# Loading the first expert tiles during the second search, and giving half of its weight splits to GpSimd, in a one-core decoder block

## The chip, the core and the metric

The kernel runs on one core of a Trainium2 chip. Its engines work beside each other, each on its own queue of instructions: TensorE (PE in the profile; PEld is its weight load), VectorE (DVE), ScalarE (ACT) and GpSimd (POOL); SyncE (SP) issues most of the plain DMA transfers and GpSimd the gathers. The metric is the time of one execution on the device in microseconds (us), lower is better. 0.3% of it is 4.9 us.

## The reference, cut to what matters

One decoder layer on 512 tokens of width 1024, in float32. Three token mixers are merged and added to x; then comes a feed-forward of 16,384 single-neuron experts, of which each token takes 128: for each of 8 heads the best 16 pairs of two 128-key halves.

```
def peer_ffn(h, w_q, keys1, keys2, u, v):
    q = (h @ w_q).reshape(B, S, PEER_HEADS, 2, half)          # 8 heads
    s1 = einsum('bshd,hkd->bshk', q[..., 0, :], keys1)        # 128 scores for each half
    s2 = einsum('bshd,hkd->bshk', q[..., 1, :], keys2)
    v1, i1 = top_k(s1, 16);  v2, i2 = top_k(s2, 16)
    cand = (v1[..., :, None] + v2[..., None, :])
    sv, si = top_k(cand, 16)
    experts = e1 * N_KEYS + e2                                # 128 of 16384 for a token
    gates = softmax(sv)
    ...
        a = einsum('cd,ced->ce', h_c, u[e_c])
        act = gelu(a) * g_c
        return einsum('ce,ced->cd', act, v[e_c])
x = x + mixers(rmsnorm(x));  x = x + peer_ffn(rmsnorm(x), ...)
```

## The kernel before, in words

**Blocks and stages.** The 512 tokens are four blocks of 128. Blocks 0 and 1 are served row by row ("rows"): for each of their 128 choices GpSimd gathers one expert row per token (an indirect DMA, L833), and a step on VectorE uses it. The table `u` gives 128 dot products for each block (L843), the table `v` adds 128 weighted rows into the block's tile `mg` (L852), so there are 512 rows. Blocks 2 and 3 are served densely: all 128 tiles of `uT` (512 KB each) are multiplied with their tokens (`dense_u`, L968, 16 matmuls of 256 columns each), ScalarE puts the gelu into a slot of the tile `ga` (L970), the gates are spread over all experts, and 128 tiles of `v` follow (`dense_v`, L142 to L144).

By the trace the stages are: the mixers of block 0 up to about 170 us; the mixers of blocks 1 to 3 up to about 640 us, with block 0's search and rows beside; the second search, for blocks 1 to 3 together, from 640 to 768 us; a stretch that I call the cover, from 768 to 859 us, in which U tiles run on TensorE while VectorE turns the search's result into weights and expert numbers and takes 36 rows; the spread of the gates, up to about 1000 us; and the tail with the 128 V tiles, the U tiles from 57 and the remaining rows.

**The second search.** It is a loop over 8 heads (`search`). Each head has two tiles of `w_pq` of 512 KB. Such a tile goes the way of `load_split`: SyncE loads it into `raw` (a ring of three), ScalarE casts the upper part `whi` (L116), then the lower part `wlo = raw - whi` is made, on VectorE (L128) or on GpSimd (L126). The number `share[0]` decides which: it is added to a running sum at each tile, and each time that the sum passes 1, GpSimd makes the tile. In the second search it is 0. Then 24 matmuls give the query `qp`, six matmuls the scores `sc` (L720), ScalarE copies them (L723), VectorE finds the best 16 of each half (L678 to L682), GpSimd adds the pairs `cand` (L689), and VectorE finds the best 16 of those one head later. The scores run two heads ahead.

Two other things are written into this loop. While its steps' assumed costs add up, every `PER_ROW` of them one row of block 0's `v` table is taken "apart": ScalarE scales the gathered row and GpSimd adds it to `mg` (L849, the second way beside L852). And 8 U tiles (`FIRST_U`) are multiplied, whose loads go through the same `raw` ring. All rows of block 0 add into one tile `mg`, so they come one after another, whichever engine adds them.

**Buffers of U.** `soon` holds the first 52 slots of `ga`, 256 numbers per partition each; a U tile is as large as four slots. U tiles from the 8th on are loaded into a ring of six (`URING`), three in `hhi` and three in `hlo`, which are free only when the search's last matmul has read them.

**Order.** Up to the end of the second search a scheduler orders the instructions of all engines by their assumed times. From the line with `manual_schedule` on, GpSimd, VectorE and TensorE run in the order in which the code is written; SyncE and ScalarE stay with the scheduler. Each engine runs its queue in order.

Of the kernel before, what the change touches and what calls it, by code (L numbers as in the profile page):

```python
# [16 lines left out]
S, D, NB, KC = 512, 1024, 4, 8  # L17
# [4 lines left out]
NK = 128  # L22
# [5 lines left out]
ND = len(DENSE)  # L28
TD = 128 * ND
FIRST_U, COVER, DURING, AFTER = 8, 24, 25, 0  # L30
KEPT = FIRST_U + COVER
SPILT = (128 - KEPT) // 3
AMONG, UNWEIGHED = 1.0, 14
LAG = FIRST_U + COVER + DURING + AFTER
GA_LATE = 6
URING, URING_V = 6, 3
# [13 lines left out]
AHEAD, ROWS_IN, MORE = 4, 5, 2  # L50
LATER = 400
PACE = {"search": 9.0, "choose": 8.0, "rows": 3.5}
EARLY_ROWS, PER_ROW = 176, 4.6


@with_exitstack
def tile_block(ctx: ExitStack, tc: tile.TileContext, t: dict, out: bass.AP):
    nc = tc.nc
# [36 lines left out]
    due, share = [0.0], [0.0]  # L95
# [3 lines left out]
    def load_raw(src, n):  # L99
        loads[0] += 1  # L100
        pool = early[0] if early and loads[0] % (RAW_MORE + 3) >= 3 else wp
        raw = pool.tile([128, WSLOT], F32, tag="raw", name="raw")
        fill(raw, src, n)
        return raw
# [107 lines left out]
    def turn(xs, g, hi, lo, dg=None, tags=("tp", "sc")):  # L212

        w = 128 * len(xs)
        for dc in range(KC):
            ps = bank(tags[dc % len(tags)])
            for b, x in enumerate(xs):
                dst, src = ps[:, b * 128:(b + 1) * 128], x[:, dc * 128:(dc + 1) * 128]
                if dg is None:
                    PE.transpose(dst, src, ident)  # L220
                else:
                    PE.matmul(dst, src, dg[:, b], start=True, stop=True)
            A.activation(hi[dc], ps[:, :w], AF.Copy, scale=g[:, dc:dc + 1])
            if lo:
                V.scalar_tensor_tensor(lo[dc], ps[:, :w], g[:, dc:dc + 1], hi[dc].bitcast(F32),
                                       op0=OP.mult, op1=OP.subtract)
# [447 lines left out]
    def search(qq, h2T, f, nb, fetch=None):  # L674

        def top16(v, i, src, n):
            tmp = qq.tile([128, 128], F32, tag="tmp", name="tmp")
            V.max(v[:, 0:8], src)  # L678
            V.max_index(i[:, 0:8], v[:, 0:8], src)
            V.match_replace(tmp[:, :n], v[:, 0:8], src, -3.0e38)  # L680
            V.max(v[:, 8:16], tmp[:, :n])
            V.max_index(i[:, 8:16], v[:, 8:16], tmp[:, :n])  # L682

        pairs = {}

        def candidates(v12):
            cand = qq.tile([128, nb, NC], F32, tag="cand", name="cand")
            for i0, ni, nj, c0 in ROWS:
                G.tensor_tensor(cand[:, :, c0:c0 + ni * nj].rearrange("p b (i j) -> p b i j", j=nj),  # L689
                                v12[:, :, 0, i0:i0 + ni, None].to_broadcast([128, nb, ni, nj]),  # L690
                                v12[:, :, 1, None, :nj].to_broadcast([128, nb, ni, nj]), op=OP.add)
            return cand

        def top_pairs(h):
            if h not in pairs:
                return
            cand = pairs.pop(h)
            for b in range(nb):
                top16(f.best[:, b, h], f.pos[:, b, h], cand[:, b], NC)
                yield 1.2  # L700

        def scores(h):
            s = []
            keys = qq.tile([128, 2, NK], F32, tag="keys", name="keys")
            nc.sync.dma_start(keys, t["keysT"][:, 2 * h:2 * h + 2])
            qp = qq.tile([128, 2, 128 * nb], F32, tag="qp", name="qp")
            if nb == 1:
                q = qq.tile([128, 256], F32, tag="q", name="q")
                gemm_plain(h2T, halves(t["w_pq"][2 * h:2 * h + 2]), 256, lambda b, ps: A.copy(q, ps), fetch)
                ps = bank("tg")  # L710
                for half in range(2):
                    PE.transpose(ps[:, half * 128:(half + 1) * 128], q[:, half * 128:(half + 1) * 128], ident)
                A.copy(qp.rearrange("p i s -> p (i s)"), ps[:, :256])
            else:
                for half in range(2):
                    A.copy(qp[:, half], gemm_tr(h2T, t["w_pq"][2 * h + half]))
            for half in range(2):
                ps = bank("sc")
                for b in range(nb):
                    PE.matmul(ps[:, b * 128:(b + 1) * 128], qp[:, half, b * 128:(b + 1) * 128], keys[:, half],  # L720
                              start=True, stop=True)
                sc = qq.tile([128, nb, NK], F32, tag="s", name="s", bufs=2 * (deep + 1))
                A.copy(sc.rearrange("p b k -> p (b k)"), ps[:, :128 * nb])  # L723
                s.append(sc)
            return s

        deep = 1 if nb == 1 else 2
        ready = [scores(h) for h in range(deep)]
        for h in range(PH):
            s = ready.pop(0)  # L730
            if h + deep < PH:
                ready.append(scores(h + deep))
            v12 = qq.tile([128, nb, 2, TOPK], F32, tag="v12", name="v12")
            for b in range(nb):
                for half in range(2):
                    top16(v12[:, b, half], f.ids[half][:, b, h], s[half][:, b], NK)
                    yield 1.6
            yield from top_pairs(h - 1)
            pairs[h] = candidates(v12)
        yield from top_pairs(PH - 1)  # L740
# [178 lines left out]
    gq, acc, late, v_raw, u_raw = {}, {}, [], {}, {}  # L919
# [4 lines left out]
        return soon[:, s] if s <= LAG - GA_LATE else late[0][:, s - (LAG + 1 - GA_LATE)]  # L924

    def fetch_u(k):
        if not FIRST_U <= k < NK:
            return
        s = (k - FIRST_U) % URING if k < LAG else (k - LAG + 1) % URING_V
        if s % BIG == 0:  # L930
            if k - FIRST_U < URING:
                u_ring[s // BIG] = by_token(wide(("hhi", "hlo")[s // BIG], BIG))
        u_raw[k] = u_ring[s // BIG][:, s % BIG]
        nc.sync.dma_start(u_raw[k], t["uT"][k])

    u_ring, u_next = [None, None], [FIRST_U]

    def fetch_u_to(k):
        while u_next[0] <= min(k, NK - 1):
            fetch_u(u_next[0])  # L940
            u_next[0] += 1
# [3 lines left out]

    def dense_u(k):

        if k < FIRST_U:
            w = load_raw(t["uT"][k], D)[:, :D]
        else:  # L950
            fetch_u_to(min(k + URING - 1, LAG + 1) if k < LAG else k)
            w = u_raw.pop(k)
        if split_u(k):
            hi, lo = (gp[0].tile([128, D], F32R, tag=tag, name=tag, bufs=1) for tag in ("uhi", "ulo"))
            A.copy(hi, w)
            yield
            V.tensor_sub(lo, w, hi.bitcast(F32))
            yield
            ps, hi, lo = bank("mm"), *(x.rearrange("p (n w) -> p n w", n=KC) for x in (hi, lo))
            for dc in range(KC):  # L960
                mm3(ps[:, :TD], (hi[:, dc], lo[:, dc]), [x[dc] for x in h2s], dc == 0, dc == KC - 1)
            A.activation(ga(k), ps[:, :TD], AF.Gelu)
            return
        w = w.rearrange("p (n w) -> p n w", n=KC)
        yield
        ps = bank("mm")
        for dc in range(KC):
            PE.matmul(ps[:, :TD], w[:, dc], h2f[dc], start=dc == 0, stop=dc == KC - 1)  # L968
            yield
        A.activation(ga(k), ps[:, :TD], AF.Gelu)  # L970
# [5 lines left out]
    with tc.tile_pool(name="qb", bufs=2) as qq:  # L976
        turn([x1[b] for b in GROUPS[1]], g2, *h2T)
        spent, dg, credit[0] = 0.0, None, 0.0
        for cost in search(qq, h2T, f, BIG):
            spent += cost  # L980
            if dg is None and spent > 12.0:
                V.tensor_copy(rstd[:, 1:NB], factors(sums, BIG))
                dg = diagonals(rstd[:, 2:NB], ND)
                turn([x1[b] for b in DENSE], g2, h2f, None, dg)
            credit[0] += cost
            while credit[0] >= PER_ROW and NJ <= done[0] < known[0]:
                credit[0] -= PER_ROW
                with tc.high_priority(-LATER):
                    step(apart=True)
            if k_u < FIRST_U and spent > 104.0 / FIRST_U * (k_u + 1):  # L990
                list(dense_u(k_u))
                k_u += 1
    assert k_u == FIRST_U, (k_u, spent)

    cp = build.enter_context(tc.tile_pool(name="cp", bufs=1))
    ctx.enter_context(tc.manual_schedule(engines={mybir.EngineType.Pool, mybir.EngineType.DVE, mybir.EngineType.PE}))
# [158 lines left out]
    while k_u < LAG:  # L1155
        list(dense_u(k_u))
        k_u += 1
    start, ready = done[0], list(operands(0))[1]
    assert start >= 2 * NJ
    nc.sync.dma_start(out[0:128], x1[0])  # L1160
# [120 lines left out]
```

## Time and profile before

| what | value |
|---|---|
| time, median of 3 runs | 1629.26 us (1627.56 to 1631.83) |
| the profiled execution: its own time | 1624.32 us |
| its span in the trace | 1622.5 us |
| busy over the span: PE / DVE / ACT / POOL | 95% / 86% / 47% / 49% |
| DMA, mean | 328 GB/s, 531.83 MB |
| mean granted TensorE clock | 0.981 |

The profiled execution is 4.9 us shorter than the median, which is 0.3%; times inside it are given from the start of its span. Rows of the timeline give start, duration, engine, line, operation, the tile written and those read, how many, and in brackets how long the engine stood idle before and what released it. A table by windows gives the busy time of each engine in each stretch of the span.

### The profile page before, as it was taken

To read this page: it belongs to the slowest core of one execution; us is meant where nothing else is said; L and a number is where in the kernel's file an instruction comes from. 1 tells how busy PE (TensorE), PEld (TensorE's weight loads), DVE (VectorE), ACT (ScalarE), POOL (GpSimd) and SP (SyncE) were. 2 spreads that over 40 slices of the span, in tenths; PEclk is the share of its full clock that TensorE was granted. 3 is DMA by queue.
4 is the path that set the end of the run, shared out by engine and by line. 5 is a ranking of instruction groups with operands and counts; after the bars stand their busy time and mean duration, and the time that the engine had idled before them with its cause. 6 is when DMAs were issued, how large, how long until landed. Compare 5 with 4: busy or idle time off the path is not lost.

```text
span 1622.5 us, 26255 instructions
## 1 busy us (share of the span) xinstructions
PE 1545.8 (95%) x8934; PEld 1382.1 (85%) x8934; DVE 1394.1 (86%) x2709; ACT 769.1 (47%) x1770; POOL 790.5 (49%) x625
## 2 busy tenths in 40 slices
PE   6999999999998989987999999899999999998998
PEld 5999899998887988987888998688888888887887
DVE  5677358899988999999998999788899888897987
ACT  7787337645445434543117878333333333333332
POOL 1100012767556555678553332566555555555652
PEclk9999999999998999999999999999999999999999
DMA  7586743899998899867997999999999999999995
GB/s 298 197 276 219 252 162 131 319 356 319 339 317 296 294 345 347 291 212 258 348 393 286 362 386 335 402 399 379 390 397 402 397 400 402 401 401 401 383 400 220
DMA packets 178101, 531.83 MB, mean 328 GB/s; under 512 B 18224, under 2 KB 47152, under 8 KB 177968
## 3 DMA queue, kind: packets, MB, share of 16 engines
q0 software_dynamic: 73728, 268.47, 44.4%
q1 hardware_dynamic: 100784, 249.12, 42.1%
q10 hardware_dynamic: 3456, 12.58, 2.0%
q8 instruction: 70, 1.15, 0.3%
q14 instruction: 63, 0.52, 0.1%
HBM read 515.42 MB, written 14.68 MB: 327 GB/s over the span
## 4 chain that ended last, share of the span: by engine, by line
PE 51%; DMA 17%; issue 14%; POOL 9%; DVE 8%; ACT 2%; SPq 0%; POOLq 0%; DVEq 0%; ACTq 0%
PE mm L968 15%; DMA row<-in_peer_v_dram,eidx 9%; POOL row L833 8%; PE mm L143 5%; PE mm L142 5%; PE mm L144 5%; DMA row<-in_peer_u_dram,eidx 3%; PE mm L295 2%; DVE wlo L128 2%; DVE scr L843 2%; PE sc L1038 2%; PE tp L1038 2%; PE sc L143 1%; PE sc L144 1%; PE tp L144 1%
## 5 line engine op out<-in xcount | busy, mean ns | idle before, releaser
L833 POOL DMA_INDIRECT row<-in_peer_v_dram,eidx x256 | 351.2, 1372 | 280.8 <-DVE mg L852 157.3
L833 POOL DMA_INDIRECT row<-in_peer_u_dram,eidx x256 | 334.9, 1308 | 266.4 <-DVE scr L843 155.0
L128 DVE TENSOR_TENSOR wlo<-raw,whi 128x1024 fp32r<-128x1024 f32 (+1 forms) x243 | 305.7, 1259 | 44.4 <-ACT whi L116 34.9
L843 DVE SCALAR_TENSOR_TENSOR scr<-row,own 128x1024 bf16<-128x1024 f32 x256 | 314.5, 1229 | 23.1 <-DMA row<-in_peer_u_dram,eidx 20.1
L852 DVE SCALAR_TENSOR_TENSOR mg<-row,acts,mg 128x1024 f32<-128x1024 f32 x237 | 304.4, 1284 | 10.7 <-DMA row<-in_peer_v_dram,eidx 6.8
L968 PE MATMUL mm<-h2f,hhi 128*128 128x256 f32 x1168 | 266.3, 379 | 0.0
L968 PEld LDWEIGHTS mm<-h2f,hhi 128*128 128x128 f32 x1168 | 218.9, 190 | 30.0
L116 ACT CAST whi<-raw 128x1024 fp32r<-128x1024 f32 (+1 forms) x148 | 154.8, 1049 | 93.7 <-PE mm L143 38.7
L189 POOL TENSOR_TENSOR rsy<-rsv,mhalf 128x4 f32<-128x4 f32 (+5 forms) x25 | 39.3, 1576 | 218.2 <-DVE rsv L188 126.2
L1084 ACT CAST whi<-raw 128x1024 fp32r<-128x1024 f32 x96 | 100.5, 1047 | 71.5 <-DMA raw<-in_peer_v_dram 50.1
L142 PE MATMUL sc<-whi,ah 128*128 128x512 f32 x256 | 110.7, 433 | 11.3 <-ACT ah L1082 6.7
L142 PE MATMUL mm<-hhi,whi 128*128 128x384 f32 x320 | 111.1, 348 | 8.0 <-ACT ga L970 6.8
L970 ACT ACTIVATE ga<-mm 128x256 f32<-128x256 f32 x95 | 36.4, 383 | 172.0 <-PE mm L968 165.7
L143 PE MATMUL mm<-hlo,whi 128*128 128x384 f32 x320 | 111.5, 348 | 0.0
L144 PE MATMUL mm<-hhi,wlo 128*128 128x384 f32 x320 | 110.6, 346 | 0.0
L142 PE MATMUL mm<-whi,hhi 128*128 128x256 f32 (+1 forms) x360 | 104.6, 292 | 3.0 <-DVE g L572 1.9
L143 PE MATMUL sc<-wlo,ah 128*128 128x512 f32 x256 | 102.2, 399 | 4.6 <-DVE wlo L128 4.6
L143 PE MATMUL mm<-wlo,hhi 128*128 128x256 f32 (+1 forms) x360 | 103.1, 287 | 0.9 <-DVE wlo L128 0.9
L1082 ACT CAST ah<-ga 128x256 fp32r<-128x256 f32 x116 | 46.7, 405 | 118.6 <-PE tp L143 73.8
L144 PE MATMUL sc<-whi,al 128*128 128x512 f32 x256 | 102.3, 399 | 0.0
L144 PE MATMUL mm<-whi,hlo 128*128 128x256 f32 (+1 forms) x360 | 101.8, 285 | 0.0
L142 PE MATMUL tp<-whi,ah 128*128 128x512 f32 x256 | 101.4, 396 | 0.0
(289 smaller groups left out, 3780.7 us busy)
## 6 DMA issues: line engine op xcount, KB each, us to landing
hhi<-in_uT_dram SPq DMA_DIRECT2D x96, 512.0 KB
raw<-in_peer_v_dram SPq DMA_DIRECT2D x96, 512.0 KB
raw<-in_w_tr_dram SPq DMA_DIRECT2D x48, 512.0 KB
raw<-in_w_nat_dram SPq DMA_DIRECT2D x40, 512.0 KB
last<-in_peer_v_dram SPq DMA_DIRECT2D x32, 512.0 KB
raw<-in_w_o_dram SPq DMA_DIRECT2D x24, 512.0 KB
hlo<-in_uT_dram SPq DMA_DIRECT2D x24, 512.0 KB
gd<-st ACTq DMA_DIRECT2D x24, 512.0 KB
```

The lines of the kernel that those rows point to most:

```text
L116: A.copy(hi[:, :n * w], raw[:, :n * w])
L128: V.tensor_sub(lo, raw, hi.bitcast(F32))
L142: PE.matmul(ps, lh, rh, start=first, stop=False)
L143: PE.matmul(ps, lh, rl, start=False, stop=False)
L144: PE.matmul(ps, ll, rh, start=False, stop=last)
L833: G.indirect_dma_start(out=r, out_offset=None, in_=t["peer_" + tab], in_offset=bass.IndirectOffsetOnAxis(ap=eidx[b][:, j:j + 1], axis=0))
L843: V.scalar_tensor_tensor(scr, r, 1.0, h2n[b], op0=OP.mult, op1=OP.mult, accum_out=acts[b][:, c]))
L852: V.scalar_tensor_tensor(x1[b], r, acts[b][:, c], x1[b], op0=OP.mult, op1=OP.add))
L968: PE.matmul(ps[:, :TD], w[:, dc], h2f[dc], start=dc == 0, stop=dc == KC - 1)
L1038: PE.matmul(ps[:, u], o[:, 1, u], o[:, 0, u], start=True, stop=True)
L1082: A.copy(ah, a)
L1084: A.copy(hi, raw)
```

## The change

Two things change, and two numbers go with them.

**U tiles.** The first 13 U tiles (`PRE_U`) no longer go through the `raw` ring and the ring of six. Each is loaded into four slots of `soon` whose activations come much later, during the second search, and is read from there by its 16 matmuls. The ring of six starts at tile 13, and its tiles are requested one earlier than before around the spread.

**Lower parts.** From the fifth head (`POOL_HEADS`) `share[0]` is 1, so GpSimd makes 8 of the 16 `wlo` of the second search. `PER_ROW` goes from 4.6 to 6.0, which writes fewer rows apart into the search.

```
+PRE_U = 13
...
-EARLY_ROWS, PER_ROW = 176, 4.6
+EARLY_ROWS, PER_ROW = 176, 6.0
+POOL_HEADS = 4
...
             else:
+                share[0] = 1.0 if h >= POOL_HEADS else 0.0
                 for half in range(2):
                     A.copy(qp[:, half], gemm_tr(h2T, t["w_pq"][2 * h + half]))
...
     def fetch_u(k):
-        if not FIRST_U <= k < NK:
+        if k < PRE_U:
+            u_raw[k] = soon[:, 4 * k:4 * k + 4].rearrange("p a b -> p (a b)")
+            nc.sync.dma_start(u_raw[k], t["uT"][k])
             return
-        s = (k - FIRST_U) % URING if k < LAG else (k - LAG + 1) % URING_V
+        s = (k - PRE_U) % URING if k < LAG else (k - LAG + 1 + (LAG - 1 - PRE_U) % URING) % URING_V
...
-        if k < FIRST_U:
-            w = load_raw(t["uT"][k], D)[:, :D]
-        else:
-            fetch_u_to(min(k + URING - 1, LAG + 1) if k < LAG else k)
-            w = u_raw.pop(k)
+        if k >= FIRST_U:
+            fetch_u_to(min(max(k, PRE_U) + URING - 1, LAG) if k < LAG else k)
+        w = u_raw.pop(k)
...
+            if u_next[0] < PRE_U and spent > 6.0 * u_next[0] + 6.0:
+                fetch_u_to(u_next[0])
...
     assert k_u == FIRST_U, (k_u, spent)
+    share[0] = 0.0
...
         list(dense_u(k_u))
         k_u += 1
+    fetch_u_to(LAG + 2)
```

The lines behind the first edits move by two or three: the L128 of before is L130 now, L833 is L836, L849 is L852, L852 is L855, the ring's load L934 is L939, and the new load is L932. GpSimd's `wlo` is L128 in the changed kernel.

What the scheduler makes of it, engine by engine. SyncE at the start of the second search, before (rows with a number are the engine's queue in order; `raw` is the ring of three):

```order
L110 DMA raw_7733<-in_w_pq_dram 128x1024
L705 DMA keys_7572<-in_keysT_dram 128x256
L705 DMA keys_7651<-in_keysT_dram 128x256
L110 DMA raw_7765<-in_w_pq_dram 128x1024
L110 DMA raw_7862<-in_w_pq_dram 128x1024
L110 DMA raw_7894<-in_w_pq_dram 128x1024
L705 DMA keys_7730<-in_keysT_dram 128x256
L110 DMA raw_8003<-in_uT_dram 128x1024
```

The first row is the fifth tile of `w_pq`, the fourth row the sixth. The first U tile stands behind the eighth. The changed kernel at the same place:

```order
L112 DMA raw_7733<-in_w_pq_dram 128x1024
L707 DMA keys_7572<-in_keysT_dram 128x256
L707 DMA keys_7651<-in_keysT_dram 128x256
L932 DMA ga_7513<-in_uT_dram 128x1024 x8
L112 DMA raw_7765<-in_w_pq_dram 128x1024
L932 DMA ga_7513<-in_uT_dram 128x1024 x5
L112 DMA raw_7859<-in_w_pq_dram 128x1024
L112 DMA raw_7891<-in_w_pq_dram 128x1024
```

Eight U loads now stand ahead of the sixth `w_pq` tile and five behind it.

SyncE at the end of the search, before (the last U tile of the `raw` ring behind the ring of six):

```order
L110 DMA raw_8797<-in_uT_dram 128x1024
L934 DMA hlo_8914<-in_uT_dram 128x1024
L934 DMA hhi_8910<-in_uT_dram 128x1024 x3
L934 DMA hlo_8914<-in_uT_dram 128x1024 x2
L110 DMA raw_8880<-in_uT_dram 128x1024
```

In the changed kernel that last row does not exist, since U tile 7 has been in `soon` from the start of the search; the six ring loads follow the last keys.

GpSimd in the middle of the search, before (`row` gathers, `mg` adds, `cand` pair sums):

```order
L849 TENSOR_TENSOR mg0_2246<-mg0_2246,row_6691 128x1024
L689 TENSOR_TENSOR cand_7854<-v12_7809 128x3x8
L689 TENSOR_TENSOR cand_7854<-v12_7809 128x3x16
L689 TENSOR_TENSOR cand_8055<-v12_7938 128x3x24
L689 TENSOR_TENSOR cand_8055<-v12_7938 128x3x16
L833 DMA row_7850<-in_peer_v_dram,eidx0_176 128x1024
L849 TENSOR_TENSOR mg0_2246<-mg0_2246,row_6694 128x1024
```

The same first add in the changed kernel:

```order
L836 DMA row_7835<-in_peer_v_dram,eidx0_176 128x1024
L852 TENSOR_TENSOR mg0_2246<-mg0_2246,row_6691 128x1024
L128 TENSOR_TENSOR wlo_8096<-raw_8092,whi_8094 128x1024
L128 TENSOR_TENSOR wlo_8224<-raw_8220,whi_8222 128x1024
L691 TENSOR_TENSOR cand_8212<-v12_8136 128x3x8
L836 DMA row_8013<-in_peer_v_dram,eidx0_176 128x1024
L691 TENSOR_TENSOR cand_8212<-v12_8136 128x3x16
L852 TENSOR_TENSOR mg0_2246<-mg0_2246,row_6694 128x1024
```

The add of `row_6691` stood ahead of the third pair sum of the first head (`cand_7854`), and now stands behind the second of the third head (ahead of the third of `cand_8212`); two `wlo` queue right behind it. Over the whole search GpSimd has 8 `wlo` more and 16 adds where it had 19; behind its last pair sum stand three gathers with their adds, where one stood.

VectorE, the last of block 0's rows that it adds itself ahead of those adds, before:

```order
L681 MAX v12_7809<-tmp_7832 128x8
L128 TENSOR_TENSOR wlo_8067<-raw_8063,whi_8065 128x1024
L852 SCALAR_TENSOR_TENSOR mg0_2246<-row_6655,acts0_177,mg0_2246 128x1024
L680 MATCH_REPLACE tmp_7838<-v12_7809,s_7643 128x128
L682 MAX_INDEX ids1_7515<-v12_7809,tmp_7832 128x8
```

And in the changed kernel:

```order
L681 MAX_INDEX ids1_7515<-v12_8136,s_7807 128x8 x2
L855 SCALAR_TENSOR_TENSOR mg0_2246<-row_6652,acts0_177,mg0_2246 128x1024
L684 MAX_INDEX ids0_7514<-v12_8136,tmp_8137 128x8
L683 MAX v12_8136<-tmp_8144 128x8
L855 SCALAR_TENSOR_TENSOR mg0_2246<-row_6655,acts0_177,mg0_2246 128x1024
L682 MATCH_REPLACE tmp_8150<-v12_8136,s_7801 128x128
```

It is the 14th row in both. It stood in the first head's best-16 work (`v12_7809`) and now stands in the third head's (`v12_8136`). GpSimd's first add, of `row_6691`, adds to the same tile right after it. Behind the search the number of rows in the cover (36) and in the spread (51) is as before, and the tail takes 233 where it took 230. TensorE has 27 U tiles behind the search's last score in both kernels.

More of the change, by code (lines that the diff above doesn't have):

```diff
@@ L926, in fetch_u @@
     def fetch_u(k):
-        if not FIRST_U <= k < NK:
+        if k < PRE_U:
+            u_raw[k] = soon[:, 4 * k:4 * k + 4].rearrange("p a b -> p (a b)")
+            nc.sync.dma_start(u_raw[k], t["uT"][k])
             return
-        s = (k - FIRST_U) % URING if k < LAG else (k - LAG + 1) % URING_V
+        s = (k - PRE_U) % URING if k < LAG else (k - LAG + 1 + (LAG - 1 - PRE_U) % URING) % URING_V
         if s % BIG == 0:
-            if k - FIRST_U < URING:
+            if k - PRE_U < URING:
                 u_ring[s // BIG] = by_token(wide(("hhi", "hlo")[s // BIG], BIG))
@@ L934, in fetch_u @@
         nc.sync.dma_start(u_raw[k], t["uT"][k])
-    u_ring, u_next = [None, None], [FIRST_U]
+    u_ring, u_next = [None, None], [0]
     def fetch_u_to(k):
```

## The prediction

> **What bounds the kernel now.** I read the table by windows first, cut at the stages' borders, then around each border the chain that ended last, the timelines and the waits.
>
> ```profile
> span 1622.5 us, 26255 instructions
> ...
> core 0: us, PE busy (x) PEld busy (x) DVE busy (x) ACT busy (x) POOL busy (x), PEclk, DMA share, GB/s
> 654.00:690.31 36.31, 35.48 (x223) 34.70 (x222) 34.88 (x113) 20.44 (x32) 20.83 (x21) 1.00 0.84 296
> 690.31:768.64 78.33, 66.20 (x358) 61.01 (x356) 76.15 (x487) 31.44 (x49) 65.55 (x60) 0.97 0.68 233
> 768.64:859.00 90.36, 89.53 (x403) 78.19 (x403) 81.46 (x129) 13.62 (x31) 51.98 (x40) 0.97 0.96 371
> 859.00:1000.00 141.00, 139.24 (x881) 129.19 (x882) 141.00 (x197) 116.36 (x460) 46.51 (x46) 1.00 0.93 346
> 1240.00:1590.00 350.00, 338.72 (x1641) 286.64 (x1640) 309.60 (x374) 126.92 (x201) 199.55 (x133) 0.99 1.03 398
> ```
>
> VectorE is full in the search (76.15 of 78.33) and in the spread (141.00 of 141). TensorE is full in the cover and nearly so in the tail (338.72 of 350), where the DMA engines are full as well. The search's end and the cover decide here. First TensorE's side of that border (issue, matmuls, pieces of the chain, ScalarE):
>
> ```profile
> 756.61 0.33 SPq L110 DMA_DIRECT2D raw<-in_uT_dram  x1
> 756.61 12.14 DMA raw<-in_uT_dram
> 756.41 0.83 PE L720 MATMUL sc<-keys,qp 128*128 128x128 f32 x6
> 757.08 7.07 PE L968 MATMUL mm<-h2f,raw 128*128 128x256 f32 x32
> 768.88 3.33 PE L968 MATMUL mm<-h2f,raw 128*128 128x256 f32 x7 [4.73 <-DMA raw<-in_uT_dram]
> 775.24 0.39 ACT L970 ACTIVATE ga<-mm 128x256 f32<-128x256 f32 x1 [2.45 <-PE mm L968]
> 778.69 0.38 ACT L970 ACTIVATE ga<-mm 128x256 f32<-128x256 f32 x1 [3.07 <-PE mm L968]
> 858.12 0.38 ACT L970 ACTIVATE ga<-mm 128x256 f32<-128x256 f32 x1 [3.07 <-PE mm L968]
> ```
>
> The last U tile in the raw ring was issued at 756.61, behind the six ring loads, and landed 12.14 us later; TensorE waited 4.73 us for it. From then to 858.12 the U tiles follow one another every 3.45 us (775.24 to 778.69). Then VectorE's side:
>
> ```profile
> 768.16 0.91 DVE L747 TENSOR_TENSOR ex<-best 128x384 f32<-128x384 f32 x1
> 774.46 1.28 DVE L852 SCALAR_TENSOR_TENSOR mg<-row,acts,mg 128x1024 f32<-128x1024 f32 x1
> 851.69 2.59 DVE L852 SCALAR_TENSOR_TENSOR mg<-row,acts,mg 128x1024 f32<-128x1024 f32 x2
> 859.00 4.62 DVE L1023 TENSOR_TENSOR o<-tg,eT 128x1024 f32<-128x1024 f32 x4 [4.72 <-ACT eT L1012]
> ```
>
> VectorE ends its cover work at 851.69 + 2.59 = 854.28 and waits 4.72 us for `eT`, which ScalarE copies behind the last gelu. So TensorE's U tiles end the cover, and VectorE is 4.7 us behind that as the next limit.
>
> **The change part by part.**
>
> *U tiles from `soon`.* Tiles 4 to 7 no longer wait for a raw buffer or stand behind the ring's loads, so the 4.73 us go. TensorE then has 27 tiles behind its last score: 27 x 3.45 = 93 us. Even from the score's old time, 756.41 + 0.83, that ends at 850.4. A second limit is ScalarE's queue: the exponential of `ex` stands there behind the gelu of tile 7, and two finished tiles can wait for it in their two `mm` banks. If `ex` comes at 767 (below) and ScalarE is past it some 5 us later, 22 tiles remain: 772 + 76 = 848. Both lie ahead of 854.28. So VectorE ends the cover, and what the removal earns is bounded by its 4.72 us, if VectorE's cover chain starts when it did.
>
> *Eight `wlo` leave VectorE.*
>
> ```profile
> L128 DVE TENSOR_TENSOR wlo<-raw,whi 128x1024 fp32r<-128x1024 f32 x8 | 17.6, 2203 | 1.7 <-ACT whi L116 1.6
> 682.16 2.42 POOL L849 TENSOR_TENSOR mg<-mg,row 128x1024 f32<-128x1024 f32 x1
> 682.47 3.25 DVE L128 TENSOR_TENSOR wlo<-raw,whi 128x1024 fp32r<-128x1024 f32 x1
> 691.92 2.84 DVE L128 TENSOR_TENSOR wlo<-raw,whi 128x1024 fp32r<-128x1024 f32 x1
> 736.39 1.20 DVE L128 TENSOR_TENSOR wlo<-raw,whi 128x1024 fp32r<-128x1024 f32 x1
> ```
>
> The group is the last eight (678 to 745 us): 17.6 us. By VectorE alone the search would end at 768.2 - 17.6 = 750.5. The long ones lie beside a GpSimd add (682.16 to 684.58 beside 682.47). The Trainium skill has the reason ("SBUF — State Buffer", section "Who interferes with whom"): VectorE and GpSimd share a port pair, which an instruction of VectorE with two SBUF inputs or one of GpSimd holds to its end. The trace agrees: 3.25 and 2.84 beside an add, 1.20 in the clear. By that rule the excess, 17.6 - 8 x 1.20 = 8.0 us, belongs to the collisions, and could return on other two-input operations; the sum would not change by it, since VectorE's limit is not the one that binds below.
>
> *Eight `wlo` come to GpSimd.* Its rows (the `wlo` is the only one it made before; then adds, gathers and pair sums of the last 78 us, and its waits):
>
> ```profile
> L126 POOL TENSOR_TENSOR wlo<-raw,whi x1: 2428/2428/2428, 193.4 to 193.4; 128x1056 fp32r<-128x1056 f32 x1
> L849 POOL TENSOR_TENSOR mg<-mg,row 128x1024 f32<-128x1024 f32 x17 | 40.7, 2395 | 0.3
> L833 POOL DMA_INDIRECT row<-in_peer_v_dram,eidx x17 | 18.7, 1098 | 4.2 <-POOL cand L689 2.5 <-POOL mg L849 1.4
> L689 POOL TENSOR_TENSOR cand<-v 128x48 f32<-128x48 f32 (+2 forms) x26 | 6.5, 266 | 8.5 <-DVE v L681 7.2 <-DVE tmp L680 1.0 <-DVE v L678 0.2
> 766.28 2.36 POOL L849 TENSOR_TENSOR mg<-mg,row 128x1024 f32<-128x1024 f32 x1
> ```
>
> The rows of `mg` are one chain. GpSimd's first add cannot run before VectorE's 14th row, and behind that add stand, to the last one: 16 adds x 2.395 = 38.3, 16 gathers x 1.098 = 17.6, 7 `wlo` x 2.43 = 17.0, 22 pair sums x 0.25 = 5.5, together 78.4; with about 3.9 us of gaps between its own instructions (2.5 + 1.4) 82.3. When does the 14th row come?
>
> ```profile
> 679.65 1.28 DVE L852 SCALAR_TENSOR_TENSOR mg<-row,acts,mg 128x1024 f32<-128x1024 f32 x1
> 695.83 0.23 POOL L689 TENSOR_TENSOR cand<-v 128x24 f32<-128x24 f32 x1 [2.16 <-DVE v L681]
> ```
>
> Before, at 679.65. In the new order it stands behind about as much of the best-16 work as VectorE had done by 695.83, but without the long `wlo` at 682.47 and 691.92, whose excess over 1.2 is 2.05 + 1.64 = 3.7: about 692.1. So the last add ends at 692.1 + 82.3 = 774.4, where it ended at 766.28 + 2.36 = 768.64. The last pair sum comes at about 763.4 (three gathers and adds earlier, 10.5 us, and a half), and `ex` some 3.2 us behind it, at 766.6; before at 768.16. The first row of the cover adds to the same tile on VectorE: it would be due 6.3 us after `ex` (774.46 - 768.16), at 772.9, but waits for GpSimd until 774.4. It was at 774.46. VectorE's cover chain therefore starts and ends as before, and the spread starts at 854.3 instead of 859.0: -4.7. In the spread both engines are full with the same work, so the gain stays.
>
> *The U loads at the search's start.* Eight of 512 KB stand ahead of the sixth `w_pq` tile. Before, that tile was issued at 644.69 and cast at 661.20:
>
> ```profile
> 644.69 0.33 SPq L110 DMA_DIRECT2D raw<-in_w_pq_dram  x1
> 661.20 1.05 ACT L116 CAST whi<-raw 128x1024 fp32r<-128x1024 f32 x1
> 663.32 1.21 DVE L128 TENSOR_TENSOR wlo<-raw,whi 128x1024 fp32r<-128x1024 f32 x1
> 650.00:655.00 5.00, 1.00 0.65 221
> 1000.00:1590.00 590.00, 570.93 (x2766) 483.38 (x2765) 515.77 (x699) 218.57 (x362) 339.21 (x226) 0.99 1.02 394
> ```
>
> 4.19 MB at 394 GB/s, the rate of full engines in the tail, are 10.6 us. The two rows of windows end with the clock, the DMA engines' share and GB/s. The engines stood at a share of 0.65 from 650 to 655, so the tile had landed by then, some 10 us ahead of its cast. The two about cancel: 0, between 0 (all hidden) and 10.6 (nothing hidden). I take 0, since the idle share shows the slack.
>
> *The tail.* Three rows more, for three fewer taken apart in the search: 3 x 512 KB at 398 GB/s = 4.0 us if the DMA engines set the end, 0 if TensorE does (338.72 of 350). I take the middle, 2.0. Tile 57's load stays at the border: 0.
>
> Sum: -4.7 + 0 + 2.0 = -2.7. The profiled execution took 1624.3, so 1621.6; it lies 4.9 under the median of the runs, and against that median the forecast is 1626.6.
>
> **The rivals.**
>
> *A (the forecast): GpSimd's queue ends the search and starts the cover.* Without the gaps the queue would end at 770.5, but the first cover row not before 772.9: -1.5; with no tail term that is -4.7 - 1.5 = -6.2. With the full tail term and the queue 2.7 us later it is +2.
>
> *B: GpSimd's queue is shorter than I sum it.* If the 14th row comes about halfway between its old time and mine, at 686, the queue ends at 768, and the first cover row comes with it: -2.7 - 6.2 = -8.9, or 1620. The floor is where the last score and the pair sums come so early that VectorE and TensorE alone set the cover: about 10 us earlier by VectorE's 750.5 with the start-up of its first rows, -4.7 - 10 + 2 = -12.7, or 1617. For it: GpSimd's row is 65.55 of 78.33, with 8.5 us of waits for VectorE that can be filled. Against: the new order puts the row in the third head's work. The Trainium skill ("Perfetto Trace Analysis", section "Optimizing Scalar/DVE Operations") says that a saturated VectorE may give work even to GpSimd, but that the shared port may leave no gain. The trace has a nearer obstacle for this case, the 82.3 us of GpSimd's queue.
>
> *C (the other side): the U loads hold up the sixth `w_pq` tile.* VectorE makes this tile's `wlo` (663.32 above), the third head's scores hang on it, and the 14th row stands behind that head's work. In the new order about as much stands ahead of this `wlo` on VectorE as before. If the cast slips by the full 10.6 us, the 14th row and the whole GpSimd queue slip by that: -2.7 + 10.6 = +7.9, or 1637. It decides from a landing later than about 661; under 2.7 us of slip it is still a gain. Against it is the 0.65 share above.
>
> *D: no difference.* Something else ends the cover at about 859, for example U tiles that ScalarE's queue holds back by 10 us more than I sum: 1629.
>
> **How the numbers follow.** 0.3% of the time, 4.9 us, is about what a measurement tells from no change. A 0.48, B 0.27, C 0.15, D 0.10. Faster by over 4.9: a quarter of A (0.12) and nearly all of B (0.24), 0.36. Slower: most of C (0.13) and a corner of A (0.03), 0.16. Within it: the rest, 0.48. The range runs from B's floor, 1617, to within C, 1635, which leaves out its upper part; A's own range, against the median, is 1623.1 to 1631.3.
>
> **What the changed profile would show.** TensorE's wait for a U tile (4.73) is gone and so is VectorE's 4.72 us ahead of the spread. GpSimd's last add ends at 774 rather than 768.6, and VectorE's first cover row begins within 1 us of it, released by GpSimd. `ex` begins at 766 to 767. GpSimd's eight `wlo` are near 2.4 us each. The sixth tile's cast lies near 661. The spread begins 4 to 5 us sooner, and the tail is 0 to 4 us longer. The forecast is wrong if the first cover row comes much before 770 (B), if the sixth cast lies beyond 665 (C), or if the spread's first instruction still waits for `eT` at 859 (D).

## The result, and the profile after

| | before | changed |
|---|---|---|
| median | 1627.63 us (8 runs) | 1637.12 us (8 runs, 1632.49 to 1640.96) |
| ratio | | 1.0055, 95% interval 1.0042 to 1.0067 |

The change makes the kernel 0.55% slower, about 9 us. The profiled execution took 1640.96 us (span 1639.2). It reached the second search 7.6 us later than that of before, although the instructions up to there are the same; a second profile of each kernel (below) shows that this is drift between executions. So I count from a mark, VectorE's first `hlo` of the second search, and give times behind it with a plus sign. The mark, before and then changed (timelines of VectorE; a row gives start, duration, engine, line, operation, tiles):

```profile
641.34 0.61 DVE L225 SCALAR_TENSOR_TENSOR hlo<-tp,gcol,hhi 128x384 fp32r<-128x384 f32 x1
```

```profile
648.96 0.61 DVE L227 SCALAR_TENSOR_TENSOR hlo<-tp,gcol,hhi 128x384 fp32r<-128x384 f32 x1
```

The changed kernel's table by windows, cut at the same times as before (7.6 us earlier in its work):

```profile
654.00:690.31 36.31, 31.44 (x194) 30.42 (x192) 27.24 (x112) 14.30 (x26) 10.71 (x14) 0.99 0.91 357
690.31:768.64 78.33, 67.99 (x385) 65.84 (x386) 67.58 (x414) 32.09 (x47) 64.87 (x58) 0.93 0.53 169
859.00:1000.00 141.00, 131.95 (x819) 121.81 (x819) 140.67 (x186) 107.26 (x418) 51.81 (x50) 0.96 0.93 349
```

VectorE, full before, has 9.1 us idle in the first window and 10.8 in the second; GpSimd is half as busy at first (10.71 where it had 20.83) while the DMA engines move more (357 GB/s, 296 before). The cause is at the search's start. Rows of SyncE's, ScalarE's, VectorE's and GpSimd's timelines, and among them one of SyncE's and one of TensorE's waits (us in all, times, longest):

```profile
648.88 8.33 SPq L932 DMA_DIRECT2D ga<-in_uT_dram  x8
658.35 0.33 SPq L112 DMA_DIRECT2D raw<-in_w_pq_dram  x1
661.73 10.58 SPq L932 DMA_DIRECT2D ga<-in_uT_dram  x5
SPq L932 <- DMA ga<-in_uT_dram: 11.9, 5, 3.0
676.93 1.04 ACT L118 CAST whi<-raw 128x1024 fp32r<-128x1024 f32 x1 [7.90 <-DMA raw<-in_w_pq_dram]
678.01 1.23 DVE L130 TENSOR_TENSOR wlo<-raw,whi 128x1024 fp32r<-128x1024 f32 x1 [5.72 <-ACT whi L118]
695.44 3.80 DVE L130 TENSOR_TENSOR wlo<-raw,whi 128x1024 fp32r<-128x1024 f32 x1
695.81 2.34 POOL L128 TENSOR_TENSOR wlo<-raw,whi 128x1024 fp32r<-128x1024 f32 x1
PE mm L146 <- DVE wlo L130: 10.5, 1, 10.5
709.49 1.26 DVE L855 SCALAR_TENSOR_TENSOR mg<-row,acts,mg 128x1024 f32<-128x1024 f32 x1
711.98 2.40 POOL L852 TENSOR_TENSOR mg<-mg,row 128x1024 f32<-128x1024 f32 x1
```

Eight U loads are issued over 8.33 us, and the sixth `w_pq` tile only behind them, at +9.4 (before +3.4). For the five behind that tile SyncE waits 11.9 us for earlier U loads to land. ScalarE waits 7.90 us for the sixth tile and casts it at +28.0, where before it did so at +19.9. VectorE stands idle for 5.72 us behind that. It makes the seventh tile's `wlo` only at +46.5 (before +25.8), and TensorE waits 10.5 us for that one. The 14th row of block 0 starts at +60.5 (before +38.3), and GpSimd's first add at +63.0 (before +40.8). What the DMA engines moved from the mark to that cast (648.9 to 677), in the view of the DMA queues; q1 carries the plain loads, q0 the gathers (packets, MB, share):

```profile
DMA packets 3193, 10.87 MB, mean 387 GB/s; under 512 B 353, under 2 KB 609, under 8 KB 3191
q1 hardware_dynamic: 2108, 6.92, 64.1%
q0 software_dynamic: 1083, 3.92, 35.7%
```

They were full or nearly so all the time (mean share 1.00); 36% of it went to the gathers. The search's end and the spread's start:

```profile
782.62 0.91 DVE L750 TENSOR_TENSOR ex<-best 128x384 f32<-128x384 f32 x1
787.60 2.90 DVE L775 TENSOR_SCALAR sh<-pos 128x128 uint32<-128x128 uint32 x1
788.05 2.36 POOL L852 TENSOR_TENSOR mg<-mg,row 128x1024 f32<-128x1024 f32 x1
791.61 1.28 DVE L855 SCALAR_TENSOR_TENSOR mg<-row,acts,mg 128x1024 f32<-128x1024 f32 x1
871.57 3.48 DVE L1029 TENSOR_TENSOR o<-tg,eT 128x1024 f32<-128x1024 f32 x3
```

The last add ends at 790.41, +141.4; the first row of the cover follows at 791.61. VectorE has no idle time just before that row: the operation at 787.60 took 2.90 us beside the last add, where before it took 0.22. The spread starts at +222.6 with no wait for `eT`. Before it was +217.7. From there to the end of the span it is 767.6 us, before 763.5.

### The profile page after: what moved, and what is told of

Its sections match the earlier page's. It is cut to its first block, busy times and chain, and to the rows that moved or that the text cites. A ratio compares the mean times of both kernels' runs of the same rounds, so it can differ in the third digit from the quotient of the medians.

```text
span 1639.2 us, 26233 instructions
## 1 busy us (share of the span) xinstructions
PE 1545.2 (94%) x8934; PEld 1383.8 (84%) x8934; DVE 1388.8 (85%) x2704; ACT 769.0 (47%) x1767; POOL 793.0 (48%) x630
## 5 line engine op out<-in xcount | busy, mean ns | idle before, releaser
L836 POOL DMA_INDIRECT row<-in_peer_v_dram,eidx x256 | 345.8, 1351 | 279.7 <-DVE mg L855 164.9
L836 POOL DMA_INDIRECT row<-in_peer_u_dram,eidx x256 | 333.6, 1303 | 267.8 <-DVE scr L846 163.6
L130 DVE TENSOR_TENSOR wlo<-raw,whi 128x1024 fp32r<-128x1024 f32 (+1 forms) x235 | 290.3, 1237 | 52.7 <-ACT whi L118 40.4
L855 DVE SCALAR_TENSOR_TENSOR mg<-row,acts,mg 128x1024 f32<-128x1024 f32 x240 | 307.5, 1281 | 13.6 <-DMA row<-in_peer_v_dram,eidx 8.8
L971 PE MATMUL mm<-h2f,hhi 128*128 128x256 f32 x1136 | 260.6, 380 | 0.0
L971 PEld LDWEIGHTS mm<-h2f,hhi 128*128 128x128 f32 x1136 | 214.3, 191 | 29.8
L146 PE MATMUL mm<-hhi,wlo 128*128 128x384 f32 x320 | 110.8, 346 | 10.5 <-DVE wlo L130 10.5
```

Source lines behind the costliest of these rows:

```text
L130: V.tensor_sub(lo, raw, hi.bitcast(F32))
L146: PE.matmul(ps, ll, rh, start=False, stop=last)
L836: G.indirect_dma_start(out=r, out_offset=None, in_=t["peer_" + tab], in_offset=bass.IndirectOffsetOnAxis(ap=eidx[b][:, j:j + 1], axis=0))
L855: V.scalar_tensor_tensor(x1[b], r, acts[b][:, c], x1[b], op0=OP.mult, op1=OP.add))
```

## The experiments

The theory after the result: the 6.8 MB of U loads at the search's start hold up the sixth `w_pq` tile; with them in view the scheduler also places VectorE's 14th row in the third head's work, and GpSimd's queue, which starts behind that row, ends late. The rival explanation: the eight `wlo` on GpSimd are what costs. Marks of all profiles, each the difference of two rows of its timelines; ratios with their 95% intervals:

| kernel | ratio | sixth cast | first add | last add ends | `ex` | spread | spread to end |
|---|---|---|---|---|---|---|---|
| before | 1 | 19.9 | 40.8 | 127.3 | 126.8 | 217.7 | 763.5 |
| before, again | | 18.7 | 39.2 | 125.9 | 125.8 | 215.4 | 762.7 |
| changed | 1.0055 [1.0042, 1.0067] | 28.0 | 63.0 | 141.4 | 133.7 | 222.6 | 767.6 |
| changed, again | | 27.3 | 62.3 | 141.2 | 133.4 | 222.3 | 767.1 |
| u_only | 1.0032 [1.0020, 1.0044] | 28.3 | 61.8 | 139.6 | 135.5 | 221.4 | 762.1 |
| wlo_rows | 0.9941 [0.9929, 0.9954] | 18.8 | 42.6 | 126.7 | 122.6 | 213.2 | 764.7 |
| tied | 0.9935 [0.9919, 0.9951] | 18.3 | 41.6 | 124.1 | 120.0 | 206.3 | 771.5 |
| rows60 | 1.0005 [0.9992, 1.0018] | 19.8 | 40.6 | 115.0 | 125.8 | 217.1 | 764.9 |
| actq | 1.0085 [1.0065, 1.0105] | 31.2 | 68.4 | 146.5 | 138.7 | 227.6 | 766.0 |
| tied_r8 | 0.9963 [0.9945, 0.9980] | 19.9 | 42.9 | 102.2 | 120.0 | 205.9 | 773.0 |
| tied_u_only | 0.9993 [0.9979, 1.0007] | 18.4 | 39.5 | 128.6 | 129.0 | 214.6 | 764.4 |
| burst_r10 | 1.0063 [1.0043, 1.0083] | 27.4 | 62.4 | 111.2 | 130.9 | 216.7 | 774.6 |
| wlo_only | 1.0016 [0.9998, 1.0035] | 18.8 | 42.2 | 137.2 | 122.1 | 217.3 | 766.8 |
| tied_half | 0.9968 [0.9956, 0.9980] | 18.8 | 42.9 | 118.2 | 121.5 | 207.4 | 767.0 |

**The U part alone, as changed (u_only).**

```
-POOL_HEADS = 4
+POOL_HEADS = 99
-EARLY_ROWS, PER_ROW = 176, 6.0
+EARLY_ROWS, PER_ROW = 176, 4.6
```

> The U part alone: 13 U tiles in the idle slots, all loaded at the search's start as in the changed kernel; no wlo on GpSimd in the search, PER_ROW 4.6 as before. Marks are counted from VectorE's first hlo of the second search (before: sixth w_pq cast +19.9, GpSimd's first add +40.8, last add ends +127.3, spread starts +217.7; changed: +28.0, +63.0, +141.5, +222.6). Theory 1 (the burst of U loads holds up the sixth w_pq tile and, in the scheduler's order, pushes VectorE's 14th row back): sixth cast at +27 to +29, first add at +58 to +64, spread starts at +218 to +222, time 1628 to 1632, ratio 1.000 to 1.003. Theory 2 (the eight wlo on GpSimd cost the time): sixth cast near +20, spread at +213, time 4 to 5 us below before, ratio 0.997.

Ratio 1.0032, just above what the theory expected; sixth cast +28.3, first add +61.8, spread +221.4. The loads alone cost time, through the same late tile and late row. But here GpSimd's queue does not end the search: the cover's first row starts 2.2 us behind the last add, 6.3 us behind `ex` as in the kernel before, so the loss is already in `ex` (+135.5, before +126.8).

**GpSimd's part alone (wlo_rows).** Before, with these edits:

```
+                share[0] = 1.0 if h >= 4 else 0.0
-EARLY_ROWS, PER_ROW = 176, 4.6
+EARLY_ROWS, PER_ROW = 176, 6.0
```

> The other part alone: eight wlo on GpSimd and PER_ROW 6.0, the U loads as before in the raw ring. Theory 1: sixth cast at +20, first add at +40 to +44, last add ends at +125 to +134; TensorE's wait for the last raw U tile stays, so the spread starts at +214 to +220; with three rows more in the tail (0 to 4 us) the time is 1625 to 1632, ratio 0.998 to 1.003. Theory 2: last add at +138 to +142, spread at +222 or later, ratio 1.004 to 1.007 like the whole change.

Ratio 0.9941, better than either theory had it. It has the sixth cast at +18.8 and the last add at +126.7. TensorE's wait for the raw U tile stays, and VectorE waits for `eT` as before:

```profile
859.55 4.62 DVE L1025 TENSOR_TENSOR o<-tg,eT 128x1024 f32<-128x1024 f32 x4 [4.34 <-ACT eT L1014]
```

So the rival explanation falls: the `wlo` on GpSimd, with fewer rows beside them, are the part that pays. The profiled execution is the slowest of its six (1626.01 against a median of 1620.01).

**The whole change with the loads spread out (tied).** From the third U tile on a one-column copy of a search result into the slot holds the load back:

```
-            if u_next[0] < PRE_U and spent > 6.0 * u_next[0] + 6.0:
-                fetch_u_to(u_next[0])
+            k = u_next[0]
+            if k < PRE_U and (k < 2 or spent > 30.0 + 5.0 * (k - 2)):
+                if k >= 2:
+                    V.tensor_copy(soon[:, 4 * k, 0:1], f.best[:, 0, int(spent / 13.2) - 2, 0:1])
+                fetch_u_to(k)
```

> The whole change, but from the third U tile on each load is tied to a result of the search (a one-column copy on VectorE into the slot ahead of the load), so that the U loads are spread over the search instead of standing ahead of the sixth w_pq tile. The 14th row is back in the first head's work in VectorE's order. Theory 1: sixth cast at +20, first add at +40 to +44, last add ends at +122 to +132, spread at +207 to +214, time 1619 to 1627, ratio 0.994 to 0.999. Theory 2: last add at +138 or later, ratio 1.003 to 1.006.

Ratio 0.9935: the same work, with the loads later, beats the kernel before. The rows that answer to those above:

```profile
646.96 0.61 DVE L227 SCALAR_TENSOR_TENSOR hlo<-tp,gcol,hhi 128x384 fp32r<-128x384 f32 x1
665.31 1.05 ACT L118 CAST whi<-raw 128x1024 fp32r<-128x1024 f32 x1
688.60 2.38 POOL L852 TENSOR_TENSOR mg<-mg,row 128x1024 f32<-128x1024 f32 x1
766.96 0.91 DVE L750 TENSOR_TENSOR ex<-best 128x384 f32<-128x384 f32 x1
853.22 4.61 DVE L1032 TENSOR_TENSOR o<-tg,eT 128x1024 f32<-128x1024 f32 x4
```

The cast waits for no transfer, the 14th row stands in the first head's work again (it starts at +35.7), GpSimd's adds start at +41.6, and the spread at +206.3, 16.3 earlier than in the changed kernel. The profiled execution is the slowest of its six (1626.51 against a median of 1617.95); whether its stretch behind the spread, 771.5, is typical no trace shows.

**PER_ROW 6.0 alone (rows60).** Before with only that number changed.

> Before with PER_ROW 6.0 alone: three rows fewer apart in the search, three more in the tail. If the tail's three rows are what costs some 4 us behind the spread in the changed kernel: spread start as before (+217 to +218), the stretch from there to the end 3 to 4 us longer, ratio 1.002. If they are hidden: ratio 0.9995 to 1.0005, and the 4 us come from the new order of the U ring at the spread.

Ratio 1.0005, spread +217.1, then 764.9, some 2 us more than before. The last add ends 12 us earlier, and `ex` and the spread stay where they were: in the kernel before, GpSimd's adds do not end the search.

**The loads on another queue (actq).** The 13 early loads are issued by ScalarE instead of SyncE (`nc.scalar.dma_start` for `nc.sync.dma_start`).

> The whole change, but the 13 early U loads are issued by ScalarE on its own DMA queue instead of SyncE's, so the sixth w_pq tile no longer stands behind them in a queue. The scheduler's order of VectorE keeps the late 14th row (third head). Marks from VectorE's first hlo of the second search (changed kernel: sixth cast +28.0, first add +63.0, last add ends +141.4, spread +222.6). If the place in SyncE's queue is what makes the sixth tile late: sixth cast +20 to +23, and the order alone leaves the first add at +49 to +54, last add ends +128 to +134, spread +213 to +218, ratio 0.998 to 1.002. If it is the bytes, whichever queue carries them: sixth cast +25 to +29, spread at +220 or later, ratio 1.003 to 1.007.

Ratio 1.0085, slower still, and not by what it was to tell apart. The issues went through so slowly that ScalarE itself stood behind them (its sequencer's issues and its own next instructions):

```profile
645.27 7.65 ACTq L932 DMA_DIRECT2D ga<-in_uT_dram  x5
652.96 0.58 ACT L225 ACTIVATE hhi<-sc,gcol 128x384 fp32r<-128x384 f32 x1 [7.12 <-issue]
652.99 5.79 ACTq L932 DMA_DIRECT2D ga<-in_uT_dram  x3
658.83 0.58 ACT L225 ACTIVATE hhi<-tp,gcol 128x384 fp32r<-128x384 f32 x1 [5.28 <-DMA ga<-in_uT_dram]
```

All that follows is late: the fifth tile's cast at +24.7 (changed: +13.6), the sixth at +31.2. So the run does not decide whether the sixth tile is late by its place in SyncE's queue or by the bytes. It shows that the burst blocks the engine that issues it. The trace of the kernel before says something on the open question: its queue of plain loads moved 0.02 MB from 650 to 651 and nothing from 651 to 655, so the sixth tile, issued at 644.69, was there some 6 us later. At that pace an issue at +9.4 would still have landed at about +16, ahead of the old cast at +19.9. By this estimate the late issue alone cost nothing, and the loads ahead of the tile and beside it made it late.

**Fewer rows apart, loads spread out (tied_r8).** tied with PER_ROW 8.0.

> The spread-out loads (tied) with PER_ROW 8.0: 10 rows apart in the search instead of 16, six more rows in the tail. In tied VectorE still waited 9.4 us for scores and 3.1 us for pair sums, which come late because GpSimd makes the wlo between its adds. If GpSimd's queue still sets the search: these waits fall below 6 us, ex comes at +113 to +117 instead of +120, spread +200 to +204, and with a hidden tail the ratio is 0.988 to 0.992; if six rows in the tail cost their bytes (3.1 MB at 398 GB/s = 7.9 us) it is 0.993 to 0.997. If GpSimd is not the limit any more: spread at +206, ratio 0.993 to 0.998.

`ex` +120.0 and spread +205.9 as in tied: there GpSimd's adds are not the limit any more. The ratio is 0.9963, the stretch behind the spread 773.0: that would fit a cost of the rows moved to the tail, but the intervals of the two ratios overlap.

**The U part alone, loads spread out (tied_u_only).** tied with POOL_HEADS 99 and PER_ROW 4.6.

> The U part alone, with the loads spread over the search; no wlo on GpSimd, PER_ROW 4.6. If the idle-slot loads do what they are for, once they do not stand ahead of the sixth tile: TensorE's wait for a U tile (4.7 us) and VectorE's 4.7 us ahead of the spread are gone, spread at +212 to +214, ratio 0.996 to 0.999. If loading into the slots costs by itself, wherever the loads stand: spread at +218 or later, ratio 1.001 or more.

Ratio 0.9993, no gain that can be told from none. The wait for `eT` is gone, but `ex` comes 2 to 3 us later, and the spread only 0.8 to 3.1 us earlier. Why `ex` is later I did not find out; VectorE's work up to it, the one-column copies included, is only about 1 us more (123.7 us, before 122.7 and 122.8).

**Before, profiled again (before_again).**

> The kernel before, profiled again, to tell how far its first profiled execution (first hlo of the second search at 641.3, spread +217.7, from the spread to the end 763.5) is typical, since the other kernels' profiled executions reach the same place 5 to 9 us later with the same instructions up to there. If that is drift between executions: the mark falls somewhere in 641 to 650, and spread minus mark stays at +217 to +219.

The mark lies at 644.04 and the marks behind it 1 to 2 us off the first profile's, which is how far two profiles of one kernel differ here. The spread, at +215.4, is earlier than I had expected.

**The burst with fewer rows on GpSimd (burst_r10).** The changed kernel with PER_ROW 10.0.

> The whole change with its burst of U loads, but PER_ROW 10: 8 rows apart in the search instead of 16, eight more rows in the tail. GpSimd's queue behind the late 14th row is 8 x 3.5 = 28 us shorter; sixth tile and order as in the changed kernel. Marks from VectorE's first hlo (changed kernel: sixth cast +28.0, first add +63.0, ex +133.7, spread +222.6; spread-out loads: +18.3, +41.6, +120.0, +206.3). If it is GpSimd's queue behind the late 14th row through which the burst costs its time: first add at +60 to +64 still, but ex at +122 to +128 and spread at +208 to +215. If the late tile costs it by itself, through VectorE's scores: ex at +131 to +134, spread at +219 to +223. The tail has eight rows more than the changed kernel and may take it back, so the time alone does not tell: 1627 to 1636.

First add +62.4 as in the changed kernel, `ex` +130.9, spread +216.7. Its rows, the wait for the tile among them:

```profile
672.27 1.04 ACT L118 CAST whi<-raw 128x1024 fp32r<-128x1024 f32 x1 [8.31 <-DMA raw<-in_w_pq_dram]
673.35 1.22 DVE L130 TENSOR_TENSOR wlo<-raw,whi 128x1024 fp32r<-128x1024 f32 x1 [6.14 <-ACT whi L118]
775.73 0.56 DVE L750 TENSOR_TENSOR ex<-best 128x384 f32<-128x384 f32 x1
861.56 4.61 DVE L1029 TENSOR_TENSOR o<-tg,eT 128x1024 f32<-128x1024 f32 x4
```

Between the two expectations. Of the 16.3 us by which the changed kernel's spread lies behind that of tied, 5.9 go when GpSimd's queue is shortened; 10.4 stay, and belong to the burst itself, by way of the tile and the order of VectorE. No run separates those two. The tables by windows, from the mark to `ex`, show where VectorE's time went, in burst_r10 and then in tied_r8, where GpSimd's adds are no limit either (behind the length of the stretch stand the busy times of PE, PEld, DVE, ACT and POOL):

```profile
644.88:775.73 130.85, 115.12 (x650) 110.61 (x651) 109.41 (x608) 44.47 (x77) 72.29 (x73) 0.93 0.68 237
642.38:762.38 120.00, 115.77 (x649) 111.69 (x650) 106.50 (x619) 46.28 (x79) 80.41 (x76) 0.94 0.74 262
```

`ex` is 10.9 us later with the burst. Of these, 7.9 are idle time of VectorE: its waits for `whi` are 6.8 us where they were 1.3, and 6.14 of them are for the sixth tile; the rest are waits for scores and pair sums. The other 2.9 are work, nearly all of it the seventh tile's `wlo`, which the new order puts beside one on GpSimd (3.80 us for 1.20).

**The eight `wlo` with all 19 rows (wlo_only).** wlo_rows with PER_ROW 4.6.

> Before with the eight wlo on GpSimd alone; PER_ROW stays 4.6, so GpSimd keeps 19 rows apart. If the 3 rows taken from GpSimd matter beside the wlo: last add at +133 to +138 and the first row of the cover waits for it, spread at +217 to +221, ratio 0.999 to 1.003. If GpSimd has room for both: like the run with both (last add +127, spread +213), ratio 0.993 to 0.996.

Ratio 1.0016. Here the forecast's mechanism stands alone, GpSimd's last add ahead of the first row of the cover:

```profile
780.43 2.35 POOL L850 TENSOR_TENSOR mg<-mg,row 128x1024 f32<-128x1024 f32 x1
782.82 1.28 DVE L853 SCALAR_TENSOR_TENSOR mg<-row,acts,mg 128x1024 f32<-128x1024 f32 x1 [3.24 <-POOL mg L850]
```

`ex` is at +122.1, as early as in wlo_rows, and yet the spread is at +217.3, since VectorE waits for the add. Three rows fewer on GpSimd decide here whether its `wlo` pay.

**One `wlo` of each head (tied_half).** tied with `share[0] = 0.5` in all heads.

> The spread-out loads, with share[0] 0.5 in all heads: the same eight wlo on GpSimd, but one of each head instead of both of the last four. In the version with the last four heads VectorE waited 9.4 us for scores, which hang on two wlo in a row on GpSimd between its adds. If that pairing makes the waits: below 5 us in all, ex at +114 to +118, spread +200 to +204, ratio 0.989 to 0.993. If not, or if the earlier start on GpSimd collides with VectorE's rows: ex at +119 to +123, ratio 0.993 to 0.997.

VectorE's waits for scores fall from 9.4 to 6.8 us and those for pair sums from 3.1 to 0.8, but `ex` is at +121.5 and the ratio 0.9968. So the pairing of the `wlo`, my reason for the waits in tied, is not what holds `ex` up.

**The changed kernel, profiled again (after_again).**

> The changed kernel, profiled again, since its first profiled execution was the slowest of its eight. If the marks are its own and not drift: sixth cast +27 to +29, first add +61 to +64, ex +133 to +135, spread +221 to +224; the first hlo of the second search falls anywhere from 641 to 650, and the stretch behind the spread is 762 to 768.

All its marks are within 0.7 us of the first profile's.

The best versions are tied and wlo_rows, 0.9935 and 0.9941, which the intervals don't tell apart; both beat the kernel before and the changed one. From the mark to the end of the span the profiled executions of before took 981.2 and 978.1 us, those of the changed kernel 990.2 and 989.4, that of wlo_rows 977.9 and that of tied 977.8. So the traces show the loss of the changed kernel in full, but of the gains of some 9 and 11 us only 0.2 to 3.4: for the size of these gains the runs' times are the only evidence.

## Why the prediction was wrong, point by point

- **The step that failed: "I take 0, since the idle share shows the slack."** The U loads' cost was put at 0 between 0 and 10.6; the sixth tile's cast slipped by 8.1 and 8.6 us in the two pairs of profiles. The idle share of 650 to 655 did show that the tile had landed early. It did not cover the burst, which I had sized at the DMA engines' full rate, 4.19 MB at 394 GB/s. The loads had 64% of it, the gathers the rest: 4.19 MB at 0.64 x 387 GB/s are by estimate 17 us, not 10.6. SyncE took 8.33 us over the eight issues, so the tile was issued 6 us later against the mark; it was there 18.6 us after its issue (658.35 to 676.93), with five more U tiles issued meanwhile. By then 6.92 MB of plain loads had gone by; without the tile itself and two tiles of keys that leaves 6.1 of the 6.8 MB of U loads, where the forecast counted only the 4.19 MB ahead of the tile. With the same loads held back (tied) the cast is at +18.3, the spread 16.3 us earlier than in the changed kernel, and the ratio 0.9935.
- **"About 692.1" for the 14th row**, in marks +50.8, fell with it: GpSimd's first add started at +63.0 and +62.3. These 12.2 us can be read off three rows, the changed kernel's from the mark to the 14th row and from the sixth tile's `wlo` to that row, and the stretch of before from which the forecast took its 692.1:

```profile
648.96:709.49 60.53, 45.92 (x259) 44.83 (x260) 51.46 (x187) 18.46 (x34) 21.62 (x26) 0.87 0.86 312
678.01:709.49 31.48, 19.06 (x108) 18.68 (x109) 31.48 (x129) 9.41 (x16) 12.36 (x17) 0.84 0.72 242
641.34:695.83 54.49, 52.46 (x309) 51.05 (x310) 52.55 (x153) 27.91 (x47) 31.08 (x27) 0.94 0.81 287
```

  VectorE was idle for 9.1 us of the first and 1.9 of the last, so 7.1 are idle time, 5.72 of it the wait for the sixth tile's cast. 2.6 are work: the forecast let the long `wlo` beside GpSimd's adds go, but the seventh tile's `wlo` now met GpSimd's own and took 3.80 us. The last 2.5 lie between the start of the 14th row and that of the add (before: 679.65 to 682.16), which the forecast's sum takes as one time. TensorE's 10.5 us wait is no part of it: from the sixth tile's `wlo` to the 14th row VectorE was never idle (31.48 busy of 31.48).
- **GpSimd's queue behind it was right**: 82.3 us forecast, 78.4 measured from the first add to the end of the last (711.98 to 790.41), 82.5 in tied. Eight `wlo` took about 2.37 us each (forecast 2.43). `ex` came 3.0 us behind the last pair sum (forecast 3.2).
- **The first row of the cover waits for GpSimd: right in that GpSimd sets its time, not in how.** It began 1.2 us behind the last add, but was not released by it. Without the 2.7 us that VectorE's operation at 787.60 lost beside the last add, the row would have come at 788.9 and waited for the add until 790.4. The spread began 79.96 us after the row (before: 79.8 of work and 4.7 of waiting). In wlo_only the wait itself is seen, 3.24 us.
- **The U wait and the wait for `eT` are gone: right** in place. But the forecast booked the 4.7 us as a gain of its own. The U part without the burst gave 0.9993, so alone they earn nothing that can be told from none.
- **The `wlo` were put too low.** The forecast let GpSimd's queue eat all that VectorE gains. That held for the late start alone. With the 14th row where it was before, the same queue ends at +124 to +127, `ex` comes 3 to 7 us earlier, and GpSimd's part alone is worth 0.59% in the runs' times.
- **The tail, 2.0 between 0 and 4.0**: the three rows alone have 764.9 (rows60) against 763.5 and 762.7, which fits the forecast but is less than profiles differ here for other reasons: wlo_only, which moves no row, has 766.8. The changed kernel's stretch is 4.1 and 4.4 longer than before's. Where that comes from stays open; u_only, with the same U loads and no row moved, has 762.1, and wlo_rows, with the same three rows, 764.7.
- **The rivals.** C is what happened in place and, less closely, in price (10.6 as an upper end, 8 measured for the tile's cast). That its time, 1637, meets 1637.12 is luck: it adds 7.9 us to 1629.3, where 9.5 were measured on 1627.6; it has the spread 5.9 us later, where the two pairs of profiles have 4.9 and 6.9, and the tail 2 longer, where they have 4.1 and 4.4. I gave C 0.15, because I read an idle share as slack for a transfer that was not yet in the picture. B's time, 1620, is about what GpSimd's part alone (1620.01) and the spread-out loads (1617.95) reach without the burst. GpSimd's queue is no shorter there (84.1 and 82.5 us from the first add to the end of the last); it starts early, which is B's condition.

The forecast cited two sections of the Trainium skill. That an instruction of VectorE and one of GpSimd hold a shared port to the end (the Trainium skill, "SBUF — State Buffer", section "Who interferes with whom") shows again here, and for an operation with one tensor input, which the section says of some copies and scalar operations in a mode that uses both ports: a 128x128 operation of VectorE took 2.90 us and ended with GpSimd's add (787.60 and 788.05 above). Whether it ran in that mode no run shows. In the kernel before, with no add beside it:

```profile
773.14 0.22 DVE L772 TENSOR_SCALAR sh<-pos 128x128 uint32<-128x128 uint32 x1
```

The doubt of the Trainium skill ("Perfetto Trace Analysis", section "Optimizing Scalar/DVE Operations") that moving work from VectorE to GpSimd may not help comes out both ways in this kernel, by the rows left on GpSimd: 1.0016 with 19, 0.9941 with 16.

## What to carry to other kernels

A load into a free place is not free: ask which transfer stands behind it or beside it, when that one is needed, and how long the issuing engine is held up; count the whole burst, and let a result of the running stage hold such loads back. Where work goes to an engine that queues behind a single row of another, the start of that row sets when the queue ends, and a scheduler that plans with the transfers may move it. And make room on the engine that takes the work: three adds fewer decided here between a gain and none.

## What the runs showed of the hardware that I had not expected

- A burst of loads blocks the engine that issues it: eight U loads kept SyncE's queue for 8.33 us, and on ScalarE thirteen of them held up three of its `hhi` writes, two of them by 7.12 and 5.28 us. It is not the issues themselves that take so long: the six ring loads of the kernel before were issued within 4 us (752.31 to 756.00). The engine waits for earlier loads to land before it issues the next; for the five U loads behind the sixth tile the profile puts 11.9 us of SyncE's waits down to that. What asks for these waits no run shows.
- VectorE's small operation with a single tensor input waited out a GpSimd add: 2.90 us for 0.22. I had looked for such collisions only where VectorE reads two tensors.
- The same instructions reach the second search at 641 to 650 us in the fourteen profiled executions, so a difference of a few us between two spans says nothing without a mark.
